# A state-space layer in an fp32 encoder kernel: an order written out by hand, splits and sums on VectorE, and rows by channel

## The chip, the cores and the metric

The kernel runs on one core of a Trainium2 chip. The metric is the device time of one execution in microseconds, as the median of several runs.

## What is computed

A trunk of two layers over a sequence of 512 positions with width 1024. Layer 0 mixes by dilated window attention, layer 1 by a bidirectional diagonal state-space layer (S5) with a gated output; after each mixer stands a SwiGLU feed-forward net, and a final RMS norm ends it. Only the second mixer is touched here:

```python
def s5_mixer(hn, w_in, a_re, a_im, log_dt, b_re, b_im, c_re, c_im, d_skip, w_glu):
    u = (hn @ w_in).reshape(b, s, SSM_GROUPS, SSM_GROUP_CH)      # 64 groups of 16 channels
    y = d_skip * u
    for direction in range(2):                                   # a scan each way, 64 complex states a group
        y = y + s5_direction(u, a_re[direction], ..., reverse=(direction == 1))
    ag = jax.nn.gelu(y.reshape(b, s, SSM_WIDTH)) @ w_glu
    return ag[..., :D_MODEL] * jax.nn.sigmoid(ag[..., D_MODEL:])
```

## The kernel before

**Matmuls.** Every fp32 weight is split into two fp32r numbers, hi and lo, and a product is made of three matmuls: hi by hi, lo by hi, hi by lo. Class `WStream` streams the weights in units of 128x1024: SP issues the load into `wraw`, three units ahead; ScalarE copies it to `whi` and `lo_engine` subtracts to get `wlo` (L108 to L117), two units ahead. `lo_engine` is VectorE, but in the state-space layer GpSimd. A unit is one DMA, except in the GLU: full units are made of four loads each (L93), half units, which hold both output parts for half of the input rows, of eight (L88).

**Tables.** The state-space layer works on chunks of eight positions, so that the recurrence over a chunk is a matmul with tables. These (`Ti` for the input, `Bt` for the output, `Mt` for what stays within a chunk, `ph` with cosine and sine of the phase) are built ahead, from about 615 to 963 us, as background pieces between the matmuls of layer 0's feed-forward net. `elem_in` (L432 to L442) makes a half tile of `Tn` in two pieces of three VectorE operations; TensorE transposes it and it goes to DRAM. The state-space layer loads the tables back, tile by tile, two buffers each.

**The state-space layer.** Eight tiles T of 128 channels (8 groups of 16). For each:

- `sps`: the projection, 24 matmuls; VectorE scales it to `u` (`s_u`, L1415); `s_move` (L1419) scatters `u` into `U` with eight 32-KB DMAs on SP, so that a group's chunk positions and channels are partitions.
- `V`: 64 small matmuls of U with `Ti` (L1308).
- `s_scan` (L1316 to L1341): four VectorE mults with `ph`, two GpSimd sums, two VectorE scans (the recurrence), four mults and two GpSimd sums, giving `xx`.
- `s_R` (L1350, L1352): four ScalarE copies of `xx` to `x`, shifted by a chunk, the second direction reversed.
- `s_O`: yps, matmuls of `Mt` with U and `Bt` with x (L1373, L1375); gelu on ScalarE (L1380).
- `s_tr`: per pair of tiles, eight transposes, then the split into `yh` and `yl`.

Then the GLU: eight output tiles of two parts. For the last four (`LATE`), `glu_part` makes the products with the first half of y while the last tiles are still in the scan, and a ScalarE copy (`gpart`, L1479) keeps them; at the end VectorE adds both halves (L1522). Gate, residual and square sums follow (L1529 to L1531, L1098 to L1101), and `msps` (L1106) begins the norm of the next feed-forward net.

The order of instructions is the order of the code on each engine; nothing is rescheduled. With V(T) the code puts the scan of T and the loads of `Ti` for T+2 on their queues; `ph`, then `Mt` and `Bt` for T+1 follow on SP behind Ti. The strides of `w_ssm_in` (channel within group outermost) are taken up when the weight is split (the `swap` units, L113 and L114).

Of the kernel before, what the change touches and what calls it, by code (L numbers as in the profile page):

```python
# [13 lines left out]
P = 128  # L14
S = 512
# [55 lines left out]
class WStream:  # L71


    def __init__(self, k, units, swap, pool, la, sa):
        self.k, self.units, self.swap, self.pool, self.la, self.sa = k, units, swap, pool, la, sa
        self.nl = self.ns = self.n = 0
        self.raw, self.hl = {}, {}
        self.lo_engine = k.nc.vector
# [21 lines left out]
    def split_to(self, n):  # L100
        nc = self.k.nc
        while self.ns <= min(n, len(self.units) - 1):
# [6 lines left out]
            if self.ns in self.swap:  # L109

                src = w.rearrange("p a (g c) -> p a c g", c=16)
                h4, l4 = (t.rearrange("p (a c g) -> p a c g", a=a, c=16) for t in (hv, lv))
                nc.scalar.activation(out=h4, in_=src, func=ACTF.Copy)  # L113
                self.lo_engine.tensor_tensor(out=l4, in0=src, in1=fv(h4), op=ALU.subtract)  # L114
            else:
                nc.scalar.activation(out=hv, in_=wv, func=ACTF.Copy)  # L116
                self.lo_engine.tensor_tensor(out=lv, in0=wv, in1=fv(hv), op=ALU.subtract)  # L117
# [63 lines left out]
class Tables:  # L181
# [5 lines left out]
    def __init__(self, k, a, cst, ident, pool, dram, rho):  # L187
# [8 lines left out]
        self.MD = [dram.tile([8, 16, 8, 128], F32, name=f"MD{t}") for t in range(KT)]  # L196
# [236 lines left out]
    def elem_in(self, T, s, i):  # L433
# [29 lines left out]
    def tr_in(self, T, s, q):  # L463
# [78 lines left out]
def build(tc, a, out):  # L542
# [45 lines left out]
    swap = range(len(units), len(units) + KT)  # L588
# [31 lines left out]
    with ExitStack() as ctx:  # L620
# [4 lines left out]
        ws = WStream(k, units, swap, wpool, 3, 2)  # L625
# [659 lines left out]
        pY = s0.enter_context(tc.tile_pool(name="psY", bufs=2, space=PSUM))  # L1285
# [30 lines left out]
        def s_scan(T):  # L1316
# [3 lines left out]
            V = vt.pop(T)  # L1320
            Vr, Vi = (V[:, i].rearrange("p g j -> p (g j)") for i in range(2))
            tl = lambda n, b=1: sp.tile([P, S], F32, tag=n, name=n, bufs=b)
            W = []
            for A_, B_, op in ((Vr, Vi, ALU.add), (Vi, Vr, ALU.subtract)):
                t1, t2 = tl("t1", 2), tl("t2", 2)
                nc.vector.tensor_tensor(out=t1, in0=A_, in1=C, op=ALU.mult)
                nc.vector.tensor_tensor(out=t2, in0=B_, in1=Sn, op=ALU.mult)
                nc.gpsimd.tensor_tensor(out=t1, in0=t1, in1=t2, op=op)
                W.append(t1)
            Q = []  # L1330
            for i in range(2):
                q = W[i]
                nc.vector.tensor_tensor_scan(out=q, data0=rho, data1=W[i], initial=0.0, op0=ALU.mult, op1=ALU.add)
                Q.append(q)
            xx[T] = []
            for i, (A_, B_, op) in enumerate(((Q[0], Q[1], ALU.subtract), (Q[1], Q[0], ALU.add))):
                x, t2 = Yp.tile([P, S], F32, tag=("sq", "acc")[i], name="xx", bufs=1), tl("t2", 2)
# [5 lines left out]
        xx = {}  # L1343

        def s_R(T):
# [9 lines left out]
            xs_[T] = R  # L1355

# [26 lines left out]
        def s_tr(t2):  # L1383
# [256 lines left out]
```

## Time and profile before

| what | value |
|---|---|
| runs | 1630.33, 1623.66, 1632.44 us; median 1630.33 |
| the profiled execution | 1624.28 us, span 1622.4 us |
| TensorE busy | 94% of the span, granted clock 0.979 on average |
| VectorE, ScalarE, GpSimd busy | 60%, 41%, 28% |
| HBM | 154 MB read, 27 MB written |

The busy shares are of the whole span; the change lies in the stretch from about 1040 to 1258 us, and in the background pieces from 615 to 963 us. The rows of those stretches follow below. A row of a wait gives who waited, on which line, for whom; a group row gives busy time, the mean of one instruction, and the idle time just before them.

### The profile page before, as it was taken

What the parts mean: (1) busy time and instruction counts of PE and PEld (TensorE: products, weight loads), DVE (VectorE), ACT (ScalarE), POOL (GpSimd) and SP (SyncE); (2) the same over time, 40 slices, a digit from 0 to 9 for tenths busy, and PEclk for the clock granted to TensorE, in tenths of its full rate; (3) what the DMA queues carried; (4) which work ended last, traced back from release to release, by engine and by line L of the source; (5) the groups of instructions that cost most, each with busy time, mean ns of one, the idle gap of its engine ahead of it and who ended that gap; (6) DMA issues with size and microseconds to landing.
All of it is one profiled execution on the core that took longest, in us unless ns stands there. A gap on an engine that the chain in (4) does not pass through costs nothing. (4 is left out here: it accounts for less than half of the span.)

```text
span 1622.4 us, 22425 instructions
## 1 busy us (share of the span) xinstructions
PE 1527.7 (94%) x8428; PEld 1261.1 (78%) x8428; DVE 976.6 (60%) x1721; ACT 660.6 (41%) x1172; POOL 452.5 (28%) x535
## 2 busy tenths in 40 slices
PE   8999999999998889799999999887799999999997
PEld 6887888898897668677777777776587888888886
DVE  6366665665666478888578875486547443344234
ACT  5265454454564323244344444442433333233122
POOL 1022001010110250387666754464413101101010
PEclk9999999999999899999999999998999999999999
DMA  6322232231222033355566547467623332333332
GB/s 185 91 78 58 62 92 64 78 87 58 90 68 66 29 86 91 84 143 146 166 194 175 163 145 253 146 223 218 210 70 88 104 103 80 104 98 98 105 102 65
DMA packets 279180, 185.16 MB, mean 114 GB/s; under 512 B 39936, under 2 KB 261280, under 8 KB 277024
## 3 DMA queue, kind: packets, MB, share of 16 engines
q1 hardware_dynamic: 278640, 183.13, 38.3%
q8 instruction: 66, 1.08, 0.3%
q10 hardware_dynamic: 432, 0.60, 0.1%
q14 instruction: 42, 0.34, 0.1%
HBM read 154.34 MB, written 27.26 MB: 112 GB/s over the span
## 5 line engine op out<-in xcount | busy, mean ns | idle before, releaser
L117 DVE TENSOR_TENSOR wlo<-wraw,whi 128x1024 fp32r<-128x1024 f32 (+1 forms) x232 | 312.1, 1349 | 192.7 <-ACT whi L116 191.0
L116 ACT ACTIVATE whi<-wraw 128x1024 fp32r<-128x1024 f32 x238 | 241.1, 1018 | 236.1 <-PE ops L1599 74.3
L789 PE MATMUL gps<-xhi,whi 128*128 128x512 f32 x792 | 320.2, 404 | 9.5 <-DVE hl L1206 6.5
L789 PE MATMUL gps<-xhi,wlo 128*128 128x512 f32 x792 | 311.9, 394 | 7.0 <-DVE wlo L117 7.0
L789 PE MATMUL gps<-xlo,whi 128*128 128x512 f32 x792 | 310.6, 392 | 0.5 <-DVE xlo L649 0.5
L983 POOL COPY st<-st 32x4 f32<-32x4 f32 x256 | 59.7, 233 | 453.9 <-ACT P L971 337.9
L789 PEld LDWEIGHTS gps<-xhi,wlo 128*128 128x128 f32 x792 | 149.3, 189 | 43.7 <-DVE wlo L117 11.2
L789 PEld LDWEIGHTS gps<-xhi,whi 128*128 128x128 f32 x792 | 149.6, 189 | 39.7 <-ACT whi L116 10.0
L789 PEld LDWEIGHTS gps<-xlo,whi 128*128 128x128 f32 x792 | 149.9, 189 | 26.0 <-DVE xlo L649 0.8
L789 PE MATMUL ups<-xhi,wlo 128*128 128x512 f32 x352 | 138.1, 392 | 2.0 <-DVE wlo L117 2.0
L789 PE MATMUL ups<-xhi,whi 128*128 128x512 f32 x352 | 139.6, 397 | 0.0
L789 PE MATMUL ups<-xlo,whi 128*128 128x512 f32 x352 | 137.7, 391 | 0.0
L971 ACT ACTIVATE P<-P,st 128x256 f32<-128x256 f32 x128 | 63.8, 499 | 68.7 <-DVE st L968 68.6
L1202 POOL TENSOR_TENSOR u<-u,g 128x512 f32<-128x512 f32 x22 | 28.4, 1291 | 209.7 <-DVE u L1200 202.2
L789 PEld LDWEIGHTS ups<-xhi,wlo 128*128 128x128 f32 x352 | 66.4, 189 | 17.0 <-DVE wlo L117 2.8
L452 POOL TENSOR_TENSOR B<-pout,C 128x512 f32<-128x512 f32 x32 | 45.3, 1415 | 122.4 <-DVE pout L178 64.3
L789 PEld LDWEIGHTS ups<-xhi,whi 128*128 128x128 f32 x352 | 66.5, 189 | 14.5 <-issue 1.2
L789 PEld LDWEIGHTS ups<-xlo,whi 128*128 128x128 f32 x352 | 66.6, 189 | 13.4
L1199 ACT ACTIVATE g<-g 128x512 f32<-128x512 f32 x44 | 27.7, 630 | 115.2 <-DVE g L1198 115.2
L789 PE MATMUL fps<-hh,whi 128*128 128x512 f32 x176 | 71.4, 406 | 3.4 <-ACT hh L1205 2.7
L891 PE MATMUL vps<-whi,xhi 128*128 128x256 f32 x256 | 73.3, 286 | 0.0
L1205 ACT ACTIVATE hh<-u 128x512 fp32r<-128x512 f32 x44 | 27.8, 633 | 109.9 <-POOL u L1202 87.7
(303 smaller groups left out, 3163.1 us busy)
## 6 DMA issues: line engine op xcount, KB each, us to landing
wraw<-in_w_ffn_in SPq DMA_DIRECT2D x88, 512.0 KB, 3.8
wraw<-in_w_qkv SPq DMA_DIRECT2D x72, 512.0 KB, 3.6
wraw<-in_w_ffn_out SPq DMA_DIRECT2D x38, 512.0 KB, 4.0
BD<-B SPq DMA_DIRECT2D x16, 512.0 KB, 5.3
TinD<-Tt SPq DMA_DIRECT2D x16, 512.0 KB, 3.5
Ti<-TinD SPq DMA_DIRECT2D x8, 1024.0 KB, 6.0
Bt<-BD SPq DMA_DIRECT2D x8, 1024.0 KB, 7.3
wraw<-in_w_attn_out SPq DMA_DIRECT2D x8, 512.0 KB, 3.8
```

The lines of the kernel that those rows point to most:

```text
L116: nc.scalar.activation(out=hv, in_=wv, func=ACTF.Copy)
L117: self.lo_engine.tensor_tensor(out=lv, in0=wv, in1=fv(hv), op=ALU.subtract)
L452: tt(out=B[:, i], in0=self.bc(self.pout, i, g0), in1=self.ch(C[:, 0]), op=ALU.mult)
L789: nc.tensor.matmul(dst, w[:, kt, :], x, start=(start and kt == ks[0] and j == 0), stop=(stop and kt == ks[-1] and j == 2))
L891: nc.tensor.matmul(ps[rp][:, r % 2, :], x, w[:, kk, :], start=(kt == 0 and j == 0 and r % 2 == 0), stop=(kt == 7 and j == 2 and r % 2 == 1))
L971: nc.scalar.activation(out=Pt[:, j, :], in_=Pt[:, j, :], func=ACTF.Exp, bias=st[:, 32 + off + j:33 + off + j], accum_out=st[:, 8 + off + j ...
L983: nc.gpsimd.tensor_copy(par[32 * z:32 * z + 32, y, :, :], own[32 * y:32 * y + 32, z, :, :])
L1199: nc.scalar.activation(out=g, in_=g, func=ACTF.Silu)
L1202: eng.tensor_tensor(out=u, in0=u, in1=g, op=ALU.mult)
L1205: nc.scalar.activation(out=hi, in_=u, func=ACTF.Copy)
```

## The change

- Weight splits stay on VectorE throughout; no `swap` units any more.
- u's rows in U run by channel, then by position in the chunk. `s_u` writes the eight positions in reverse, `s_move` has one DMA for each group (so V of a group needs one DMA only), and the tables are laid out to match: `elem_in` writes `Tn` with the position innermost and reads `pin` (a power of the state matrix, position outermost in memory) with a step of 512 bytes.
- `s_scan` is cut into `s_pre` and `s_post`; three of its four sums are on VectorE, some second operands lie in PSUM (`pU`), and only the second x sum is on GpSimd.
- `ph` of T+2 is loaded by ScalarE's DMA queue at the end of `s_R(T)`; Ti of T+2 is issued right after V(T); Mt and Bt of T+2 after the moves.
- The calls stand in one list. Transposes are made in two halves with one bank of PSUM and copied back in place. Six output tiles of the GLU instead of four are half done ahead, cut in parts between the other steps.

The core of the diff (the added scaling of `first`, the GLU banks and plain renamings are left out):

```diff
-            if self.ns in self.swap:
-                src = w.rearrange("p a (g c) -> p a c g", c=16)
...
+            nc.scalar.activation(out=hv, in_=wv, func=ACTF.Copy)
+            self.lo_engine.tensor_tensor(out=lv, in0=wv, in1=fv(hv), op=ALU.subtract)
...
-        tt(out=o, in0=self.bc(self.pin, 0, g0), in1=self.ch(bb[:, i]), op=ALU.mult)
-        tt(out=t, in0=self.bc(self.pin, 1, g0), in1=self.ch(bb[:, 1 - i]), op=ALU.mult)
+        pw = [self.pin[:, :, j, g0:g0 + 4].rearrange("p l (g o) -> p g o l", o=1).to_broadcast([P, 4, 16, 8]) for j in range(2)]
+        b = [bb[:, j].rearrange("p g (c o) -> p g c o", o=1).to_broadcast([P, 4, 16, 8]) for j in range(2)]
+        tt(out=o, in0=pw[0], in1=b[i], op=ALU.mult)
+        tt(out=t, in0=pw[1], in1=b[1 - i], op=ALU.mult)
...
-    LATE = range(4, KT)
+    LATE = range(2, KT)
...
-        def s_scan(T):
+        def s_pre(T):
...
             for A_, B_, op in ((Vr, Vi, ALU.add), (Vi, Vr, ALU.subtract)):
-                t1, t2 = tl("t1", 2), tl("t2", 2)
+                t1 = sp.tile([P, S], F32, tag="t1", name="t1", bufs=2)
+                t2 = pU.tile([P, S], F32, tag="t", name="t2p")
                 nc.vector.tensor_tensor(out=t1, in0=A_, in1=C, op=ALU.mult)
                 nc.vector.tensor_tensor(out=t2, in0=B_, in1=Sn, op=ALU.mult)
-                nc.gpsimd.tensor_tensor(out=t1, in0=t1, in1=t2, op=op)
...
+            for t1, t2, op in W:
+                nc.vector.tensor_tensor(out=t1, in0=t1, in1=t2, op=op)
+            for t1, _, _ in W:
+                nc.vector.tensor_tensor_scan(out=t1, data0=rho, data1=t1, initial=0.0, op0=ALU.mult, op1=ALU.add)
...
+        def s_post(T):
...
-                nc.gpsimd.tensor_tensor(out=x, in0=x, in1=t2, op=op)
+                (nc.vector, nc.gpsimd)[i].tensor_tensor(out=x, in0=x, in1=t2, op=op)
...
+            if T + 2 < KT:
+                load_tab(T + 2, "ph", eng=nc.scalar)
...
-            nc.vector.tensor_tensor(out=us[T], in0=ps, in1=rB, op=ALU.mult)
+            nc.vector.tensor_tensor(out=bass.AP(tensor=u.tensor, offset=u.offset + 448, ap=[list(u.ap[0]), [-64, 8], [1, 64]]),
+                                    in0=v(ps), in1=v(rB), op=ALU.mult)
...
-                nc.sync.dma_start(out=Us[T % 3][112 - 16 * l:128 - 16 * l, :, 1:65], in_=us[T][:, 64 * l:64 * l + 64])
+                nc.sync.dma_start(out=Us[T % 3][:, g, 1:65], in_=us[T][16 * g:16 * g + 16].rearrange("c (l j) -> c l j", l=8))
...
+        run((s_su, 2), (s_move, 2), (s_g, 3, 0), (s_V, 0), (s_pre, 0), (s_g, 3, 1), (s_su, 3), (s_post, 0), (s_V, 1), (s_pre, 1),
+            (s_g, 4), (s_su, 4), (s_g, 5), (s_R, 0), (s_O, 0), (s_post, 1), (s_V, 2), (s_pre, 2), (s_su, 5),
+            (s_g, 6), (s_R, 1), (s_O, 1), (s_post, 2), (s_V, 3), (s_pre, 3), (s_su, 6),
+            (s_tr, 0, 0), (s_g, 7, 0), (s_tr, 0, 1), (s_g, 7, 1), (s_R, 2), (s_O, 2), (s_post, 3),
+            (s_V, 4), (s_pre, 4), (s_su, 7), (s_R, 3), (s_O, 3), (s_V, 5), (s_tr, 1, 0), (s_tr, 1, 1),
+            (s_post, 4), (s_pre, 5), (next, fill[0]), (next, fill[0]), (next, fill[1]), (s_R, 4), (s_O, 4),
+            (s_V, 6), (s_post, 5), (s_pre, 6), (next, fill[1]), (next, fill[2]), (s_R, 5), (s_O, 5), (s_V, 7),
+            (s_tr, 2, 0), (next, fill[2]), (s_tr, 2, 1), (s_post, 6), (s_pre, 7), (next, fill[3]), (s_R, 6), (s_O, 6),
+            (s_post, 7), (next, fill[3]), (next, fill[4]), (next, fill[4]),
+            (s_R, 7), (s_O, 7), (next, fill[5]), (s_tr, 3, 0), (next, fill[5]), (s_tr, 3, 1))
```

Three places show how the instructions moved. **VectorE, the scan of tile 1**, before (`t` are the scan's operands, `xx` its result):

```order
L1415 TENSOR_TENSOR u<-sps_9704,rsB_9588 128x512
L1326 TENSOR_TENSOR t_9777<-V,ph 128x512
L1327 TENSOR_TENSOR t_9778<-V,ph 128x512
L1326 TENSOR_TENSOR t_9782<-V,ph 128x512
L1327 TENSOR_TENSOR t_9783<-V,ph 128x512
L1333 SCALAR_TENSOR_TENSOR t_9777<-rr_9494,t_9777 128x512
L1333 SCALAR_TENSOR_TENSOR t_9782<-rr_9494,t_9782 128x512
L1338 TENSOR_TENSOR xx<-t_9777,ph 128x512
L1339 TENSOR_TENSOR t_9790<-t_9782,ph 128x512
L1338 TENSOR_TENSOR xx<-t_9782,ph 128x512
L1339 TENSOR_TENSOR t_9795<-t_9777,ph 128x512
```

and now, where `t2p` is an operand in PSUM:

```order
L1322 TENSOR_TENSOR t_9776<-V,ph 128x512
L1323 TENSOR_TENSOR t2p<-V,ph 128x512
L1322 TENSOR_TENSOR t_9780<-V,ph 128x512
L1323 TENSOR_TENSOR t2p<-V,ph 128x512
L1327 TENSOR_TENSOR t_9776<-t_9776,t2p 128x512
L1327 TENSOR_TENSOR t_9780<-t_9780,t2p 128x512
L1329 SCALAR_TENSOR_TENSOR t_9776<-rr_9497,t_9776 128x512
L1329 SCALAR_TENSOR_TENSOR t_9780<-rr_9497,t_9780 128x512
L110 TENSOR_TENSOR wlo<-wraw,whi 128x1024
L1427 TENSOR_TENSOR u<-sps_9794,rsB_9591 128x8x64
L110 TENSOR_TENSOR wlo<-wraw,whi 128x1024
```

The two sums (L1327) are now between the mults and the scans, and two weight splits (`wlo`) and the scaling of a later tile stand between the scans and the mults behind them, which before came at once.

**SP, the queue around the loads for tile 5**, before (`wraw` are half units of the GLU, `U<-u` moves):

```order
L88 DMA wraw<-in_w_glu 64x2x128 x8
L1251 DMA Ti<-TinD_5462 128x2048
L1251 DMA ph<-PhD_5477 128x1024
L1419 DMA U_9486<-u 16x8x64 x8
L1251 DMA Mt<-MD_5485 128x1024
L1251 DMA Bt<-BD_5469 128x2048
```

and now, at the same number of moves:

```order
L88 DMA wraw<-in_w_glu 64x2x128 x8
L1433 DMA U_9488<-u 128x1x64 x8
L1246 DMA Mt<-MD_5484 128x1024
L1246 DMA Bt<-BD_5468 128x2048
L1246 DMA Ti<-TinD_5462 128x2048
L88 DMA wraw<-in_w_glu 64x2x128 x8
```

`ph` has left the queue, and `Ti` of tile 5 (TinD_5462) now comes behind the moves of tile 4 and the tables Mt and Bt of tile 3 instead of ahead of moves and tables.

**ScalarE around the copies of tile 4**, before (`x<-xx` are the copies, `rr` an operand of the scan of a later tile):

```order
L116 ACTIVATE whi<-wraw 128x1024
L1391 ACTIVATE yh_10332<-yt 128x512
L1391 ACTIVATE yh_10336<-yt 128x512
L1350 ACTIVATE x_10340<-xx 64x512
L1352 ACTIVATE x_10340<-xx 64x512
L1350 ACTIVATE x_10343<-xx 64x512
L1352 ACTIVATE x_10343<-xx 64x512
L1314 ACTIVATE rr_9494<-rho 128x8x63
```

and now:

```order
L1394 ACTIVATE ys<-yt 128x512 x2
L1400 ACTIVATE yh_10369<-ys 128x512
L1400 ACTIVATE yh_10373<-ys 128x512
L109 ACTIVATE whi<-wraw 128x1024
L1457 ACTIVATE gpart<-pe 128x512 x2
L109 ACTIVATE whi<-wraw 128x1024
L1457 ACTIVATE gpart<-pe 128x512
L1352 ACTIVATE x_10470<-xx 64x512
L1354 ACTIVATE x_10470<-xx 64x512
L1352 ACTIVATE x_10473<-xx 64x512
L1354 ACTIVATE x_10473<-xx 64x512
L1246 DMA ph<-PhD_5479 128x1024
```

Now two weight copies and three copies of half tiles stand ahead of the x copies, and the load of ph behind them.

## Rows read from the trace of the kernel before

**Rows 1.** busy time by stretch, 1040 to 1240; stretch, its length, busy us (x instructions) by engine, PEclk, DMA share, GB/s

```profile
1140.00:1160.00 20.00, 12.42 (x101) 10.07 (x102) 12.98 (x15) 5.62 (x10) 12.50 (x8) 0.83 0.78 248
...
sum 200.00, PE 170.56 PEld 142.56 DVE 118.44 ACT 71.53 POOL 77.59; mean PE 17.06 PEld 14.26 DVE 11.84 ACT 7.15 POOL 7.76
```

**Rows 2.** waits of TensorE, 1020 to 1265: total us, times, longest us

```profile
PE yps L1375 <- ACT x L1352: 17.8, 12, 5.3
PE pe L789 <- ACT gpart L1479: 7.6, 1, 7.6
PE V L1308 <- DMA U<-u: 3.5, 1, 3.5
```

**Rows 3.** VectorE's groups, 1040 to 1180: busy us, mean ns, idle before and releasers

```profile
L1333 DVE TENSOR_TENSOR_SCAN t<-rr,t 128x512 f32<-128x512 f32 x16 | 26.8, 1713 | 9.9 <-ACT rr L1314 5.1 <-POOL t L1328 4.7
L1339 DVE TENSOR_TENSOR t<-t,ph 128x512 f32<-128x512 f32 x16 | 19.5, 1220 | 0.0
L1326 DVE TENSOR_TENSOR t<-V,ph 128x512 f32<-128x512 f32 x16 | 10.9, 683 | 20.6 <-DMA ph<-PhD 16.6 <-PE V L1308 4.0
...
L1338 DVE TENSOR_TENSOR xx<-t,ph 128x512 f32<-128x512 f32 x16 | 10.7, 669 | 0.0
```

**Rows 4.** waits of ScalarE, 1040 to 1180

```profile
ACT whi L116 <- DMA wraw<-in_w_glu: 31.1, 4, 13.1
```

**Rows 5.** SP's DMA issues in order of time: start, us, engine, line

```profile
1090.64 8.85 SPq L88 DMA_DIRECT2D wraw<-in_w_glu  x8
1099.59 0.54 SPq L1251 DMA_DIRECT2D Ti<-TinD  x1
1100.22 0.38 SPq L1251 DMA_DIRECT2D ph<-PhD  x1
```

**Rows 6.** the page's costliest groups: VectorE's weight splits

```profile
L117 DVE TENSOR_TENSOR wlo<-wraw,whi 128x1024 fp32r<-128x1024 f32 (+1 forms) x232 | 312.1, 1349 | 192.7 <-ACT whi L116 191.0
```

**Rows 7.** groups of GpSimd and ScalarE, 1040 to 1180

```profile
L1340 POOL TENSOR_TENSOR xx<-xx,t 128x512 f32<-128x512 f32 x16 | 22.8, 1423 | 34.1 <-DVE t L1339 33.3 <-PE sps L789 0.7
...
L1352 ACT ACTIVATE x<-xx 64x512 f32<-64x512 f32 x16 | 10.0, 627 | 0.2
```

**Rows 8.** TensorE in order of time: start, us

```profile
1177.75 1.07 PE L1375 MATMUL yps<-Bt,x 128*64 128x128 f32 x8
...
1179.66 0.39 PE L789 MATMUL pe<-yh,wlo 128*128 128x512 f32 x1
1179.89 0.40 PE L789 MATMUL pe<-yh,whi 128*128 128x512 f32 x1
...
1183.30 1.03 PE L1386 MATMUL yt<-cst,ys 128*128 128x128 f32 x8
...
1223.63 0.39 PE L789 MATMUL pg<-yh,whi 128*128 128x512 f32 x1
...
1257.89 1.05 PE L1106 MATMUL msps<-ones,acc 128*128 128x1 f32 x8 [1.56 <-POOL acc L1101]
```

**Rows 9.** VectorE in order of time, the GLU's half tiles

```profile
1229.76 1.27 DVE L1522 TENSOR_TENSOR gpart<-pg,gpart 128x512 f32<-128x512 f32 x2
...
1237.04 1.27 DVE L1522 TENSOR_TENSOR gpart<-pg,gpart 128x512 f32<-128x512 f32 x2
...
1251.59 1.27 DVE L1522 TENSOR_TENSOR gpart<-pg,gpart 128x512 f32<-128x512 f32 x2
```

**Rows 10.** VectorE's groups, 640 to 1000: a table mult

```profile
L440 DVE TENSOR_TENSOR Tn<-pin,bbP 128x512 f32<-128x512 f32 x32 | 21.7, 678 | 0.4 <-ACT bb L431 0.4
```

**Rows 11.** VectorE in order of time: a plain and a strided weight split

```profile
1000.42 1.22 DVE L117 TENSOR_TENSOR wlo<-wraw,whi 128x1024 fp32r<-128x1024 f32 x1 [1.36 <-ACT whi L116]
...
1023.95 1.98 DVE L114 TENSOR_TENSOR wlo<-wraw,whi 128x1024 fp32r<-128x1024 f32 x1 [0.96 <-ACT whi L113]
```

**Rows 12.** busy time by stretch, 615 to 800 and 800 to 963, summed

```profile
sum 348.00, PE 331.62 PEld 259.75 DVE 281.47 ACT 136.73 POOL 206.06; mean PE 165.81 PEld 129.87 DVE 140.74 ACT 68.37 POOL 103.03
```

**Rows 13.** waits of TensorE, 640 to 1000

```profile
PE gps L789 <- DVE wlo L117: 5.5, 7, 1.7
```

More of the change, by code (lines that the diff above doesn't have):

```diff
@@ L195, in __init__ @@
         self.PhD = [dram.tile([P, 2, S], F32, name=f"PhD{t}") for t in range(KT)]
-        self.MD = [dram.tile([8, 16, 8, 128], F32, name=f"MD{t}") for t in range(KT)]
+        self.MD = [dram.tile([16, 8, 8, 128], F32, name=f"MD{t}") for t in range(KT)]
         self.z, self.C = {}, {}
@@ L606, in glu_half @@
                       for u in range(2) for g in range(2) for part in range(2)])
-    LATE = range(4, KT)
+    LATE = range(2, KT)
     for m in LATE:
         glu_half(m, 0)
-    for m in range(4):
+    for m in range(LATE[0]):
         glu_full(m)
@@ L1326, in s_scan @@
                 nc.vector.tensor_tensor(out=t1, in0=A_, in1=C, op=ALU.mult)
                 nc.vector.tensor_tensor(out=t2, in0=B_, in1=Sn, op=ALU.mult)
-                nc.gpsimd.tensor_tensor(out=t1, in0=t1, in1=t2, op=op)
[L1329 to L1334, printed above, removed]
+                W.append((t1, t2, op))
@@ L1335, in s_scan @@
+            vt.pop(T)
+            for t1, t2, op in W:
+                nc.vector.tensor_tensor(out=t1, in0=t1, in1=t2, op=op)
+            for t1, _, _ in W:
+                nc.vector.tensor_tensor_scan(out=t1, data0=rho, data1=t1, initial=0.0, op0=ALU.mult, op1=ALU.add)
+            Qs[T] = [w[0] for w in W]
+        def s_post(T):
+            ph = ld[T]["ph"]
+            C, Sn = ph[:, 0, :], ph[:, 1, :]
+            Q = Qs.pop(T)
             xx[T] = []
             for i, (A_, B_, op) in enumerate(((Q[0], Q[1], ALU.subtract), (Q[1], Q[0], ALU.add))):
[L1337 removed]
+                x = Yp.tile([P, S], F32, tag=("sq", "acc")[i], name="xx", bufs=1)
+                t2 = sp.tile([P, S], F32, tag="t2", name="t2", bufs=2) if i else pU.tile([P, S], F32, tag="t", name="t2p")
@@ L1411, in build, with s_V, s_O @@
+        def s_V(T):
+            s_rho(T)
+            for g in range(8):
+                s_v(T, g)
+            if T + 2 < KT:
+                load_tab(T + 2, "Ti")
+        def s_O(T):
+            for q in range(4):
+                s_out(T, q)
+            s_gelu(T)
+            if T + 3 < KT:
+                s_move(T + 3)
+            if T + 2 < KT:
+                load_tab(T + 2, "Mt", "Bt")
         us = {}
@@ new lines, in s_move, with s_g @@
+        def s_move(T):
+            for g in range(8):
+                nc.sync.dma_start(out=Us[T % 3][:, g, 1:65], in_=us[T][16 * g:16 * g + 16].rearrange("c (l j) -> c l j", l=8))
+        gps, rB = {}, []
+        def s_g(T, part=None, hook=None):
+            if part != 1:
+                gps[T] = (ws.get(), (pT if T == 2 else p1).tile([P, S], F32, tag="yt" if T == 2 else "f", name="sps2"))
+            wl, ps = gps[T]
+            ks = {None: range(KT), 0: range(KT // 2), 1: range(KT // 2, KT)}[part]
+            gemm_a(Z, ps, wl=wl, ks=ks, start=part != 1, stop=part != 0, hook=hook)
```

191 lines of the change are left out of this document (58 added, 133 removed).

## The prediction

> **What bounds it now.** I read the page's first table (TensorE busy 94% of the span), then busy time by stretch. Outside the state-space stage TensorE hardly pauses. Inside it, from 1040 to 1180, its busy time falls to 12.42 of 20 us and its granted clock to 0.83 [rows 1]: the lower of its two levels, 1.2 GHz, for part of the stretch, right after it had stood idle. The sum over 1040 to 1240 is 170.56 us busy in 200, so 29.4 us of TensorE stand still.
>
> The waits of TensorE say for what: 17.8 us for the state copies x that ScalarE makes, in 12 pieces (5.3 us the longest), 7.6 us once for a half-tile copy, 3.5 us once for moved u [rows 2]. The copies are only the last link. One step back, on VectorE, the first mult of a tile's scan waited 16.6 us for `ph`, in four pieces, 5.1 us for `rr` from ScalarE and 4.7 us for a sum from GpSimd [rows 3]. On ScalarE a weight copy waited 31.1 us for its load, with rr and x queued behind it [rows 4]. Both start at SP: at 1090.64 eight GLU loads take 8.85 us to issue, then come Ti and, only at 1100.22, ph [rows 5]. So the stage is bound by a chain SP, VectorE, GpSimd, ScalarE, TensorE, once per tile.
>
> **The change, term by term.** Let X be the end of the last tile's yps: before, 1177.75 + 1.07 = 1178.8 [rows 8].
>
> 1. *ph from ScalarE's queue.* It is issued behind the x copies of two tiles earlier, so a tile ahead of its use. The 16.6 us should go. ScalarE pays six issues; none of its issues is in the trace, so each costs between 0 and SP's 0.38 [rows 5], at most 2.3 us. They stand ahead of the gelu, which waits for yps anyway, so I cost them at nothing; without that cover it is the 2.3 us.
>
> 2. *Splits and sums on VectorE.* What the chain then costs is VectorE's own time per tile. From rows 3: before the split point four mults with V (0.68 each, starts 0.60 apart in a row), two sums taken as such an op, two scans of 1.71: 6 x 0.61 + 3.43 = 7.1 us. After it four mults and one sum at 0.61 to 0.67, about 3.2 us. L1339 means 1.22 beside L1338's 0.67: the second of each tile shares its time with a GpSimd sum, and with three of four sums gone from GpSimd I count it at 0.67 for most. Per tile that is 10.3 us, for eight 82 us. To this come eight weight splits between the scans of tile 0 and the last x (the order on VectorE, above, shows two of them), at 1.35 [rows 6], 10.8 us; five u at 0.68, 3.4 us; six yl, also 0.68, 4.1 us. Together 100 us. V(0)'s 3.5 us wait [rows 2] should go, since each group's V waits for its own move only and half a projection stands ahead of it; so VectorE can begin near 1052. 1052 + 100 = 1152; one GpSimd sum of 1.4, two x copies of 0.63 [rows 7] and the outputs (four blocks like the last of rows 8, some 2.5) give **X = 1158** if VectorE never waits. That is the lower end.
>
> 3. *The new waits.* The upper end is X = 1178, where it stands. ScalarE's 31.1 us of waiting for GLU loads [rows 4] is not removed: the half units come through SP as eight loads each, six of them before X instead of four, at 8.85/8 = 1.1 us per load where the lanes are full [rows 5]. In the new order the copies of such units stand on ScalarE ahead of the x copies of tiles 4 and 6, and half-tile copies ahead of those of tiles 4 to 7. SP's own list loses six ph issues (2.3 us) and gains 16 loads before X. So one or two of these late weights will still push a tile. Nothing in the trace says by how much; I take the middle, **X = 1168**, a gain of 10.8 us. What else is moved past SP (moves by channel, eight of 32 KB as before; Ti now ahead of the moves) I cost at nothing: its cover is the two-tile lead, and if that is gone a move is a V wait like the 3.5 us above.
>
> 4. *Six half tiles.* After X TensorE has the sixth half tile, the last transposes and the GLU: four full tiles and four halves before, two full and six halves now. A half tile is 24 matmuls of 0.227 (the starts of two neighbours in rows 8), 5.45 us, a full one 10.9. But half tiles leave VectorE and ScalarE only every 1237.04 - 1229.76 = 7.28 us [rows 9], so from the second on this sets the pace. From X: 5.45 + 1.0 (transposes, rows 8) + 21.8 for the full ones; 6.2 to the first half tile's sum (its first matmul began at 1223.63 [rows 8], the sum at 1229.76); 5 x 7.28 to the sixth's; and 1257.89 - 1251.59 = 6.3 [rows 8, 9] to the square sum `msps`. Together 77.2 us; before it was 1257.89 - 1178.8 = 79.1. Gain **1.9 us**: two half tiles are off TensorE there, 10.9 us, and the chain eats most. The copies that the transposes gain (0.6 us each, like the x copies) lie on this path for the last pair alone, under the sixth half tile; without that cover they are 1.2 us more.
>
> 5. *Rows by channel.* The eight strided weight splits become plain ones; they gave TensorE no wait. The table-building pieces pay instead: 64 VectorE mults, now 0.68 [rows 10], read `pin` with a 512-byte step in the innermost axis. The nearest row is VectorE's strided split of weights, 1.98 us beside 1.22 for the plain one [rows 11]: 0.76 more for 1024 elements, 0.38 for 512. 64 x 0.38 = 24 us more VectorE work, in a stretch where it is busy 281 of 348 us [rows 12]. Lower bound 0 (the other operand is a broadcast, which may leave room), upper bound 24, all of it exposed. Most is hidden, since TensorE's weights are split two units ahead; what isn't hidden is what delays a split that is late already: TensorE waited 5.5 us for them in seven pieces [rows 13]. Two pieces of table, four strided mults, stand ahead of a split at most, 1.5 us. I take **3 us**, two such waits lengthened.
>
> Sum: -10.8 - 1.9 + 3 = -9.7 on the profiled 1624.28 gives 1614.6. That execution lies near the lowest of the runs shown; with them (1623.66, 1630.33, 1632.44) the mean of four is 1627.7, 3.4 above it. So I forecast **1618 us**. The median of 1630.33 less 0.5% (8.2 us, about what a measurement can tell from no change) is 1622.2.
>
> **The rivals.**
>
> A. *VectorE is the only bound.* X = 1158 and no table cost: -20.8 - 1.9 = -22.7, with 3.4 again 1605. For it: the ph wait is the largest single one and plainly goes. Against: 31.1 us of late weights.
>
> B. *The late weight takes ph's place.* SP is issuing back to back, so the x copies of tiles 4 to 6 stand behind GLU loads as scan mults waited for ph. X = 1177, and the table costs its 3 us: -1.8 - 1.9 + 3 = -0.7: 1627. For it: one cause, SP, stood behind both waits. Against: ph no longer stands in that queue, and the order puts plain work ahead.
>
> C. *The strided table reads come out.* Each strided mult is 0.38 longer, so each block of two pieces (there are 16) delays the split behind it by 1.5 us, and TensorE waits as much more wherever the split had no slack. It decides from 0.75 us a block: 16 x 0.75 = 12 us is the 3.7 us of gain with X near 1177, and 8.2 over. At 1.0 us a block it is 1627.7 - 3.7 + 16 = 1640; with X = 1168 it is 1631. For it: VectorE is busy 81% of that stretch, and splits are late seven times already. Against: these waits sum to 5.5 us today, and splits are made two units ahead.
> The Trainium skill ("Advanced Engine Details and Errata", section Memory Cachelines) says that SBUF reads which hit a different 16-byte line at each access pay a penalty; that speaks against this change. The trace agrees in kind: 1.98 against 1.22 us [rows 11]. The page gives no size, so the sum goes by the row.
>
> D. *The change does not shorten the chain*: TensorE's written-out order itself waits, for instance a half tile for its one psum copy as in the 7.6 us [rows 2]. It gives B's time, and I count it there.
>
> **Chances.** Forecast (X between 1163 and 1173): 0.38. A: 0.19. B with D: 0.26. C: 0.17. Faster by over 0.5%: all of A and three quarters of the forecast, 0.47. Within 0.5%: the rest of the forecast and B, 0.35. Slower: C's, with the end of B, 0.18. The range goes from a little under A, for the spread of the runs, 1602, to between C's two times, 1636. The likeliest case alone spans 1613 to 1623.
>
> **What would show it.** Right: no wait of VectorE's scan mult for ph; GpSimd's share down by the splits and three sums; last yps near 1168; half tiles every 7.3 us to the end; table mults near 1.06 us. Wrong: yps still waiting some 15 us for x with whi behind in_w_glu (B); TensorE waits for wlo between 640 and 1000 above 15 us (C); TensorE never below 18 of 20 us in the stage (A).

## The result, and the profile after

The changed kernel takes 1678.52 us (median of four runs, 1670.69 to 1678.94) beside 1629.88 for the kernel before (now four runs): a ratio of 1.0301, with a 95% interval of 1.0275 to 1.0326. It is 49 us slower; the forecast was 1618, with a range from 1602 to 1636. The profiled execution took 1678.76 us, its span is 1677.0.

To see where the time went I cut both traces at four instructions: the first hh copy of layer 0's feed-forward net (hh is the hi part of its hidden values), the first V, the end of the last yps, and msps after the GLU. What comes before the first differs by at most 5.3 us between all these executions, what comes behind the last by 1.7. The later runs stand in the same table (their edits are told below); the ratio is to runs of the kernel before on the same chip.

| kernel | hh to first V: tables, projections | V to last yps: scan stage | to msps: tail | ratio (95%) |
|---|---|---|---|---|
| before | 433.4 | 128.7 | 79.1 | 1 |
| after | 456.7 | 147.5 | 89.4 | 1.0301 (1.0275 to 1.0326) |
| e1 pin plain | 438.6 | 145.5 | 89.3 | 1.0193 (1.0166 to 1.0220) |
| e2 before, strided | 455.1 | 123.9 | 79.2 | 1.0126 (1.0101 to 1.0151) |
| e3 adds behind | 451.6 | 142.9 | 77.2 | 1.0225 (1.0192 to 1.0258) |
| e4 half tiles' splits late | 456.4 | 139.7 | 90.1 | 1.0275 (1.0249 to 1.0302) |
| e5 splits on GpSimd | 453.1 | 149.7 | 90.2 | 1.0315 (1.0291 to 1.0340) |
| e6 ph on SP | 450.3 | 150.0 | 90.1 | 1.0311 (1.0284 to 1.0339) |
| e7 post first | 453.0 | 146.0 | 90.9 | 1.0288 (1.0254 to 1.0323) |
| e8 all splits late | 458.6 | 145.6 | 89.5 | 1.0296 (1.0262 to 1.0329) |
| e9 Ti behind | 451.5 | 145.8 | 89.4 | 1.0296 (1.0266 to 1.0327) |
| c1 five edits | 436.1 | 133.8 | 77.0 | 1.0044 (1.0027 to 1.0061) |
| c2 and post of tile 4 first | 436.5 | 133.1 | 77.0 | 1.0041 (1.0026 to 1.0057) |
| c3 c1 with four halves | 438.8 | 127.4 | 80.4 | 1.0039 (1.0025 to 1.0052) |
| e10 MD on GpSimd | 460.1 | 142.7 | 90.2 | 1.0319 (1.0294 to 1.0343) |
| c4 c1, MD on GpSimd | 445.2 | 133.4 | 77.3 | 1.0068 (1.0045 to 1.0092) |
| c5 before, MD on GpSimd | 444.6 | 128.9 | 78.8 | 1.0068 (1.0044 to 1.0092) |
| e11 MD stores later | 449.4 | 145.1 | 89.4 | 1.0275 (1.0243 to 1.0306) |
| c6 c1, MD stores later | 431.5 | 133.8 | 77.5 | 1.0000 (0.9986 to 1.0015) |
| c7 before, MD stores later | 427.8 | 125.3 | 78.8 | 0.9954 (0.9937 to 0.9970) |

A column is one execution. Stretches of the same code differ between executions: the first one takes 450 to 459 us where nothing in it was edited (after, e3, e4, e6 to e9), the second 143 to 148 (after, e1, e3, e10, e11). So a column shows what a stage lost only to within 5 to 8 us, and a verdict on less is the ratio's. One execution of e9 took 3054.72 us at full clock, for no reason that the record shows; its ratio rests on the other three.

All three stretches are longer: +23.3, +18.8 and +10.3. Of the first, 2.7 us are work that was moved in, the half projection that now stands ahead of V(0) (12 matmuls of 0.227). In that stretch the table mults answer to [rows 10]; the groups of VectorE, 640 to 1040, of the changed kernel:

```profile
L436 DVE TENSOR_TENSOR Tn<-pin,bbP 128x512 f32<-128x512 f32 x32 | 34.6, 1081 | 0.5 <-ACT bb L424 0.5
L437 DVE TENSOR_TENSOR tm<-pin,bbP 128x512 f32<-128x512 f32 x32 | 34.3, 1073 | 0.0
```

1.08 us against 0.68, 32 of each. TensorE's waits between 690 and 1040, after the change (total us, times, longest; gps and fps are the feed-forward net's gate and output matmuls, tps and eps those of the tables):

```profile
PE gps L784 <- DVE wlo L110: 7.2, 6, 1.9
PE gps L784 <- ACT whi L109: 5.2, 3, 3.4
PE fps L784 <- DVE wlo L110: 4.0, 5, 1.3
PE fps L784 <- ACT whi L109: 3.6, 4, 1.5
PE fps L784 <- ACT hh L1200: 3.2, 1, 3.2
PE tps L466 <- DVE Tn L438: 2.4, 2, 2.2
PE eps L475 <- ACT Tt L467: 1.9, 2, 1.0
```

and in the same part of the program (690 to 1025) of the kernel before, those for split weights:

```profile
PE gps L789 <- DVE wlo L117: 3.7, 4, 1.7
PE fps L789 <- DVE wlo L117: 2.9, 3, 1.1
...
PE gps L789 <- ACT whi L116: 1.2, 1, 1.2
PE fps L789 <- ACT whi L116: 0.6, 1, 0.6
```

In all the kernel before waits 11.3 us there, 6.6 of them for wlo and 1.8 for whi, the copy on ScalarE; here it is 27.5, with 11.2 for wlo and 8.8 for whi.

In the scan stage no wait for ph is left: the first mults of the scans wait for V alone ([rows 3] have 16.6 us for ph):

```profile
L1322 DVE TENSOR_TENSOR t<-V,ph 128x512 f32<-128x512 f32 x16 | 10.9, 683 | 7.7 <-PE V L1304 7.7
```

The waits of TensorE from 1060 to 1330 ([rows 2]):

```profile
PE yps L1380 <- ACT x L1354: 34.0, 14, 10.5
PE pg L784 <- DVE gpart L1501: 14.1, 2, 8.4
```

The waits for x have doubled, from 17.8 to 34.0. The two longest are one place each. ScalarE in order of time (the idle time before an instruction, and what ended it, stands in brackets):

```profile
1099.36 1.06 ACT L109 ACTIVATE whi<-wraw 128x1024 fp32r<-128x1024 f32 x1 [7.13 <-DMA wraw<-in_w_ssm_in]
...
1100.32 0.61 ACT L1352 ACTIVATE x<-xx 64x512 f32<-64x512 f32 x1
...
1168.09 1.06 ACT L109 ACTIVATE whi<-wraw 128x1024 fp32r<-128x1024 f32 x1 [10.23 <-DMA wraw<-in_w_glu]
...
1169.53 0.62 ACT L1352 ACTIVATE x<-xx 64x512 f32<-64x512 f32 x1
```

and SP's issues ahead of the first of them:

```profile
1087.73 1.00 SPq L1246 DMA_DIRECT2D Ti<-TinD  x2
1088.85 0.38 SPq L96 DMA_DIRECT2D wraw<-in_w_ssm_in  x1
```

The last projection's weight is issued at 1088.85, behind two Ti of 1 MB; it lands 10.4 us later, the copy whi runs at 1099.36, and only then x of tile 0: TensorE stood still for 7.0 us. At 1168.09 it is a GLU half unit in front of tile 4's x, and TensorE stood still for 10.5 us.

Busy time by stretch (length, busy us of TensorE, its weight loads, VectorE, ScalarE and GpSimd, granted clock, DMA share, GB/s), from the first V to the last yps and from there to msps, of the changed kernel:

```profile
1076.00:1224.00 148.00, 111.08 (x1151) 93.17 (x1152) 90.98 (x126) 50.94 (x78) 10.23 (x8) 0.86 0.57 184
1224.00:1313.00 89.00, 74.91 (x316) 60.99 (x314) 48.79 (x50) 27.18 (x36) 19.60 (x15) 0.90 0.23 66
```

and of the kernel before:

```profile
1050.00:1179.00 129.00, 103.60 (x1137) 87.22 (x1138) 84.20 (x93) 47.16 (x70) 63.01 (x40) 0.90 0.67 206
1179.00:1258.00 79.00, 76.51 (x339) 62.78 (x340) 46.60 (x47) 26.56 (x33) 19.61 (x15) 1.00 0.28 81
```

TensorE is idle for 36.9 us of the stage (148 - 111.08), 25.4 before: 11.5 of the 18.8 us. 2.7 are work that was moved in, a fifth half tile (5.45) less the half projection that now stands ahead of V(0) (2.7). The rest, 4.6 us, I put down to the clock: a mean granted clock of 0.86 beside 0.90 means some 41 us at the lower level, 1.2 GHz (2 x 0.14 x 148), beside 26, in a stage with more stops. VectorE is busy 61% of it; e5, below, takes the splits off it and wins nothing.

The tail has 5.45 us of work less (the sixth half tile ahead is in it) and is 10.3 longer: TensorE is idle for 14.1 us of it beside 2.5, and the clock is 0.90 beside 1.00. Its half tiles ([rows 9]), VectorE:

```profile
1257.73 1.27 DVE L1501 TENSOR_TENSOR gpart<-pg,gpart 128x512 f32<-128x512 f32 x2
...
1264.97 0.68 DVE L1501 TENSOR_TENSOR gpart<-pg,gpart 128x512 f32<-128x512 f32 x1
1270.83 0.69 DVE L1501 TENSOR_TENSOR gpart<-pg,gpart 128x512 f32<-128x512 f32 x1 [5.18 <-PE pg L784]
...
1277.53 1.27 DVE L1501 TENSOR_TENSOR gpart<-pg,gpart 128x512 f32<-128x512 f32 x2
```

and TensorE there:

```profile
1265.71 0.79 PE L784 MATMUL pg<-yh,whi 128*128 128x512 f32 x1 [5.72 <-DVE gpart L1501]
...
1292.78 0.80 PE L784 MATMUL pg<-yh,whi 128*128 128x512 f32 x1 [8.37 <-DVE gpart L1501]
```

At 1264.97 one add stands alone, the second follows at 1270.83: from 1264.97 to the next tile's adds at 1277.53 it is 12.6 us instead of 7.28, and once more, with the wait at 1292.78, 12.7.

### The profile page after: what moved, and what is told of

Read it like the earlier page. It is cut to its first block, busy times and chain, and to the rows that moved or that the text cites. A ratio compares the mean times of both kernels' runs of the same rounds, so it can differ in the third digit from the quotient of the medians.

```text
span 1677.0 us, 22457 instructions
## 1 busy us (share of the span) xinstructions
PE 1546.1 (92%) x8428; PEld 1272.8 (76%) x8428; DVE 1009.7 (60%) x1760; ACT 660.6 (39%) x1184; POOL 388.5 (23%) x500
## 3 DMA queue, kind: packets, MB, share of 16 engines
q8 instruction: 66, 1.08, 0.3%
## 5 line engine op out<-in xcount | busy, mean ns | idle before, releaser
L110 DVE TENSOR_TENSOR wlo<-wraw,whi 128x1024 fp32r<-128x1024 f32 (+1 forms) x245 | 327.8, 1342 | 224.2 <-ACT whi L109 222.6
L109 ACT ACTIVATE whi<-wraw 128x1024 fp32r<-128x1024 f32 x246 | 249.5, 1019 | 256.9 <-PE ops L1578 74.3
L1194 ACT ACTIVATE g<-g 128x512 f32<-128x512 f32 x44 | 27.7, 630 | 128.9 <-DVE g L1193 128.9
L784 PE MATMUL fps<-hh,wlo 128*128 128x512 f32 x176 | 70.2, 399 | 5.5 <-DVE wlo L110 5.5
L1201 DVE TENSOR_TENSOR hl<-u,hh 128x512 fp32r<-128x512 f32 x44 | 35.8, 813 | 63.4 <-ACT hh L1200 63.4
```

The costliest lines, as they stand in the source:

```text
L784: nc.tensor.matmul(dst, w[:, kt, :], x, start=(start and kt == ks[0] and j == 0), stop=(stop and kt == ks[-1] and j == 2))
L1194: nc.scalar.activation(out=g, in_=g, func=ACTF.Silu)
L1201: nc.vector.tensor_tensor(out=lo, in0=u, in1=fv(hi), op=ALU.subtract)
```

## The experiments

**Theory 1: the strided reads.** e1 stores pin with the position innermost, by the same instructions:

```diff
-        self.pin, self.pout = self.t("pin", [8, 2, 64]), self.t("pout", [8, 2, 64])
+        self.pin, self.pout = self.t("pin", [2, 64, 8]), self.t("pout", [8, 2, 64])
...
-            V.tensor_copy(self.pin[0:64, 1:8, i, :], pw[i][0:64, 0:7])
+            V.tensor_copy(self.pin[0:64, i, :, 1:8].rearrange("p g l -> p l g"), pw[i][0:64, 0:7])
...
-        pw = [self.pin[:, :, j, g0:g0 + 4].rearrange("p l (g o) -> p g o l", o=1).to_broadcast([P, 4, 16, 8]) for j in range(2)]
+        pw = [self.pin[:, j, g0:g0 + 4, :].rearrange("p g (o l) -> p g o l", o=1).to_broadcast([P, 4, 16, 8]) for j in range(2)]
```

> The changed kernel with pin stored position innermost, so that the 64 table mults read it with a step of one element; everything else as changed. Theory 1 (the strided reads cost what was lost before 1040 us: 64 mults at 1.08 instead of 0.68 us, nothing of it hidden): mults back at 0.68 us and about 25 us less, near 1654. Rival 1 (the reads were hidden, and what was lost there comes from something else in rows by channel, the transposes or the table DMAs): mults at 0.68 us, time within 5 us of 1678.

Measured: the mults take 0.68 us again:

```profile
L436 DVE TENSOR_TENSOR Tn<-pin,bbP 128x512 f32<-128x512 f32 x32 | 21.7, 678 | 0.5 <-ACT bb L424 0.5
```

The time is 1658.83 us; the ratio falls by 0.0108, 17.6 us. e2 puts the strided operands (the added lines of elem_in in the change, written into the old tile) into the kernel before:

> The kernel before with only the operands of the 64 table mults changed to the strided ones; the order of the table's elements is then another one than the rest of the kernel takes, so the layer's values differ, not its work. Theory 1: mults at 1.08 us and 20 to 25 us more than before, near 1652. Rival 1: within 5 us of 1630.

Measured: 1645.62 us, 1.26% or 20.5 us more than before, all in the first stretch (+21.7). Its two groups of mults:

```profile
L443 DVE TENSOR_TENSOR Tn<-pin,bbP 128x512 f32<-128x512 f32 x32 | 34.5, 1079 | 0.5 <-ACT bb L431 0.5
L444 DVE TENSOR_TENSOR tm<-pin,bbP 128x512 f32<-128x512 f32 x32 | 34.4, 1075 | 0.0
```

So one and the same part is worth 18 us taken away and 20 added. 25.2 us of work were added on VectorE (68.9 for the two groups less 43.7 with plain reads), and 70 to 80% of it is paid. Theory 1 stands, rival 1 is out; the size was 7 us under what e1 expected and at the lower end for e2.

**Theory 2: the adds.** For output tiles 3 and 6 both parts lie in one PSUM tile (pV), and the code wrote the add of part 0 ahead of the matmuls of part 1. e3:

```diff
                 for part in range(2):
                     gemm_a(Yl[4:], pp[part], wl=tuple(w[:, :, part * 128:part * 128 + 128] for w in wl), ks=range(4))
+                for part in range(2):
                     t = parts.pop((m, part))
                     nc.vector.tensor_tensor(out=t, in0=pp[part], in1=t, op=ALU.add)
```

> The changed kernel with both matmul groups of a half tile written ahead of its two adds. Theory 2 (for output tiles 3 and 6, whose two parts lie in one PSUM tile, the second group waits for the first add: TensorE's waits of 5.7 and 8.4 us for gpart): half tiles every 7.3 us throughout, about 10.5 us less, near 1668. Rival 2 (VectorE's and ScalarE's chain of 7.3 us sets the end anyway, and the waits lie beside it): under 3 us less.

Measured: 1663.54 us, 0.0076 or 12 us less (10.5 expected); the tail is 77.2 us. VectorE's adds:

```profile
1248.38 1.27 DVE L1502 TENSOR_TENSOR gpart<-pg,gpart 128x512 f32<-128x512 f32 x2
...
1255.65 1.27 DVE L1502 TENSOR_TENSOR gpart<-pg,gpart 128x512 f32<-128x512 f32 x2
...
1262.93 1.27 DVE L1502 TENSOR_TENSOR gpart<-pg,gpart 128x512 f32<-128x512 f32 x2
```

Every step is 7.28 us now, and both waits for gpart are gone. Nothing but the place of the adds was changed, so what the matmuls of part 1 waited for was the add that reads part 0 of the same tile, though the two parts share no word.

**Theory 3: late weights in ScalarE's queue.** e4 splits the half tiles' weights one unit ahead instead of two:

```diff
-            hi, lo = ws.get()
+            hi, lo = ws.get(ahead=1)
```

> The changed kernel with the weights of the half tiles done ahead split one unit ahead instead of two, so that a late GLU load no longer stands on ScalarE in front of the x copies of tile 4. Theory 3 (late weights in the in-order queues are what the scan stage lost: TensorE's longest wait for x, 10.5 us at 1170, goes): 8 to 12 us less, near 1668. Rival 3 (the tile is late for another reason, Ti or the moves, and the wait only changes its name): within 3 us of 1678. Slower is possible too if TensorE then waits for splits: up to 5 us more.

Measured: the wait of 10.5 us at tile 4 is gone, the stage 7.8 us shorter in its profile; 1672.23 us, a ratio 0.0026 lower, 4 us with intervals that overlap. That the late unit caused this wait is shown; that it cost the 8 to 12 us expected is not. e8 does the same with the last three projections (`ws.get(ahead=1 if T > 4 else None)`):

> The run with the half tiles' weights split one unit ahead, and the last three projections' weights too, so that no late weight copy stands on ScalarE in front of the x copies of tile 0. Theory 3: TensorE's first long wait for x (7 us) goes as the second did, and the stage from the first V to the last yps is near the 129 us of before: 15 to 18 us less than the change, near 1661. Rival 6 (tile 0's x are late by the scan, not by the weight): the wait stays, near 1672.

Measured: both long waits are gone, TensorE's sum for x falls to 16.7 us, and the time stays (1.0296), where 15 to 18 us less were expected. In their place stand 5.3 us for a wlo that is now split too late and 6.2 for U: TensorE's waits in the stage fall only from 37.0 to 32.0 us in all. e9 takes the other end, the order on SP:

```diff
+            if 1 < T and T + 2 < KT:
                 load_tab(T + 2, "Ti")
...
-            (s_g, 4), (s_su, 4), ...
+            (s_g, 4), (load_tab, 2, "Ti"), (load_tab, 3, "Ti"), (s_su, 4), ...
```

> The changed kernel with the loads of Ti for tiles 2 and 3 (1 MB each) behind the load of the last projection's weight instead of ahead of it on SP; nothing else. Theory 3: that weight landed 10.4 us after its issue because of them, and its copy stands on ScalarE in front of tile 0's x; TensorE's wait there falls from 7.0 to 1 or 2 us, 4 to 6 us less in the stage. Rival 7: the weight is as late with the loads in the other order, or V(2) now waits for Ti: within 3 us of 1678.

Measured: tile 0's wait goes, and one of 6.8 us appears two tiles later, behind the copy of the next late GLU unit; 1.0296. A late transfer that is mended shows the next: the order holds several in a row, and no one of these three runs gives time clear of its interval.

**Rival 4 (VectorE's splits hold up the scan), and the other parts.** e5 sets `ws.lo_engine = nc.gpsimd` again for the stage:

> The changed kernel with the weight splits of the state-space stage (from projection 0 to the last half tile ahead) on GpSimd again. Theory 3 (late weight copies on ScalarE stand in front of x; the split behind them on VectorE is only in their wake): the waits of 7.0 and 10.5 us for x stay, 1678 within 4 us. Rival 4 (the split on VectorE, which waits for its weight copy, holds up the scan queued behind it): TensorE's waits for x shrink by 8 us or more in all and the time with them.

Measured: 1.0315, waits for x 31.4 us with 9.7 the longest. Having the splits on VectorE neither helped nor hurt here. e6 leaves out `eng=nc.scalar`:

> The changed kernel with ph loaded on SP's queue again, at the same place of the code. If loading by ScalarE is what took VectorE's waits for ph away, they come back in part, a few us to 10 us more. Rival: the place in the code (two tiles ahead) did it, not the queue: no wait for ph, within 3 us of 1678; and if the load on ScalarE's queue itself delayed the gelu, up to 4 us less.

Measured: VectorE waits for ph again, and the time is the same (1.0311 beside 1.0301):

```profile
DVE t L1322 <- DMA ph<-PhD: 12.7, 3, 5.8
```

In the changed kernel, which waits elsewhere, the wait for ph is covered. Whether it was covered in the kernel before too no run shows: none loads ph by ScalarE's queue there, or by SP's in c1. e7 moves `(s_post, 6), (s_pre, 7)` ahead of `(s_tr, 2, 0)`:

> The changed kernel with s_post and s_pre of tiles 6 and 7 ahead of the transposes of pair 2, so that yl on VectorE stands behind them and not in front; TensorE's own order is the same. Theory 5 (VectorE waited 11.1 us in front of yl at 1196 with the ready x of tile 6 behind it): x of tile 6 earlier by 8 to 10 us, and TensorE's waits at 1200 to 1203 (5.0 us) go: 3 to 6 us less. Rival: TensorE reaches tile 6's outputs no earlier, since half tiles fill its queue: within 2 us of 1678.

Measured: the waits of 2.8 and 2.2 us at tile 6 become 1.5 and 0.9, but the time is within its interval (1.0288): not settled.

**Together.** c1 has the edits of e1, e3, e4, e7 and e9.

> The changed kernel with all five edits: pin position innermost, both matmul groups of a half tile ahead of its adds, half tiles' weights split one unit ahead, post of tile 6 ahead of pair 2's transposes, Ti of tiles 2 and 3 behind the last projection's weight. If the three losses (table reads, late weights, adds) are separate, they add: 18 to 23 + 12 + 8 to 15 us less than 1678, so 1628 to 1640. If they hide one another, it stays above 1645.

Measured: 1632.88 us, 1.0044 (1.0027 to 1.0061): 42 of the 49 us are back, within what was expected if the three losses add. Stage and tail are 133.8 and 77.0. e1 and e3 alone gave 17.6 and 12.4 us, so by subtraction the three edits of the order gave some 12 together, an estimate that the intervals leave open by 9 either way. The busy time of c1's stage, and TensorE's waits for x:

```profile
1053.00:1187.00 134.00, 109.30 (x1150) 91.80 (x1148) 89.83 (x125) 49.79 (x77) 10.23 (x8) 0.90 0.64 199
```

```profile
PE yps L1380 <- ACT x L1354: 21.4, 14, 6.3
```

TensorE is idle for 24.7 us of it, beside 25.4 before, and waits 21.4 us for x, beside 17.8: even mended, the new order has none of the gain for which it was written. The longest wait, 6.3 us, is the late GLU unit that e9 brought up at tile 2. c2 also moves `(s_post, 4)` ahead of `(s_tr, 1, 0)`:

> The run with all five edits, and post of tile 4 ahead of pair 1's transposes, so that yl of pair 1 no longer stands before it on VectorE. If what is left of tile 4's wait comes from VectorE's order, 2 to 4 us less than with the five edits; if from SP's queue, no difference.

No difference. c3 has `LATE = range(4, KT)` and the calls of two fills left out:

> The run with all five edits, and four half tiles done ahead instead of six. Theory: two half tiles more are 10.9 us of TensorE moved from the tail, where the 7.3-us chain of VectorE and ScalarE takes most of it back, into the stage, where part of it falls into waits: with four, the tail is 5 to 8 us longer and the stage about as much shorter: within 4 us of the five edits. Rival: six halves fill waits that stay empty with four: 5 us or more slower with four.

Measured: 6.5 us less in the stage, 3.4 more in the tail (5 to 8 were expected), 1.0039: within the interval of c1. No gain of six halves over four is seen.

**By which route the tables' delay reaches TensorE (theory 8: through SP's queue).** SP waits 124.8 us in front of the MD stores between 690 and 1040 (102.6 before), for VectorE, and weight loads queue behind. e10, c4 and c5 issue those 64 stores from GpSimd's queue (`self.nc.gpsimd.dma_start`) in the changed, the mended and the kernel before:

> The changed kernel with the 64 stores of the within-chunk table (MD) issued from GpSimd's queue instead of SP's. Theory 8 (the late VectorE reaches TensorE by way of SP: the store waits for E on VectorE, the weight load queued behind it is late, and so is ScalarE's copy): TensorE's waits for whi and wlo between 690 and 1050 fall by 8 us or more, 8 to 15 us less than the change. Rival 8 (the split itself stands behind the mults on VectorE): waits for wlo stay, under 4 us less.

> The run with all five edits, and the 64 stores of MD on GpSimd's queue. If the same route costs something with plain table reads too, 3 to 8 us less than with the five edits, so at or below the kernel before; if VectorE in time leaves SP nothing to wait for, no difference.

> The kernel before with nothing but the 64 stores of MD on GpSimd's queue. Theory 8: its 7 us of waits for split weights between 690 and 1025 shrink, 2 to 6 us less than before. Rival 8: no difference; GpSimd's own issue of them could cost 1 or 2 us.

What theory 8 forecast came in none of the three: they take 1.0319, 1.0068 and 1.0068, that is 3, 4 and 11 us more than without the edit (the first two within their intervals). In e10 TensorE's waits for whi and wlo between 690 and 1040 did fall, from 20.0 to 7.7 us, but 11.7 us for the copy of a transposed table (Tt) and 5.4 for hl, the lo part of the hidden values, came up. GpSimd itself now waits in the stores for VectorE (86.2 us in e10), and SP waits for GpSimd's ph (72.9 us, 5.7 before the edit). The wait only changed its queue. e11, c6 and c7 leave the queue and move the stores behind weight loads:

```diff
-                u += behind[3:]
+                u += behind[3:4]
...
+                u += behind[4:]
                 u.append((400, lambda T=T, s=s: self.store_out(T, s)))
```

> The changed kernel with the MD stores four pieces later in the background list, still on SP, so that one or two weight loads a half block stand ahead of them and no longer behind; engines, their orders and the work are otherwise the same. Theory 8 (SP waits in the store for VectorE and holds up the weight load behind it): SP's waits in front of MD fall below half of 125 us, TensorE's waits for whi and wlo between 690 and 1050 shrink by 8 us or more, 8 to 15 us less than the change. Rival 8 (the split itself stands behind the longer mults on VectorE): SP's waits fall, TensorE's don't, within 4 us of the change.

> The run with all five edits, and the MD stores later. Theory 8: 3 to 8 us less than with the five edits, near or below the kernel before (ratio 0.998 to 1.002). Rival 8: no difference (1.004).

> The kernel before with nothing but the MD stores later. Theory 8: its waits for split weights between 690 and 1025 shrink, 3 to 6 us less than before (ratio 0.996 to 0.998). Rival 8: no difference.

Measured: e11 takes 0.0026 less than the change, 4 us with intervals that overlap. SP's waits in front of the MD stores fall from 124.8 to 76.2 us, not below half. Its waits of TensorE from 690 to 1040 are

```profile
PE eps L475 <- ACT Tt L467: 9.4, 5, 2.9
PE fps L785 <- DVE wlo L110: 3.1, 4, 1.5
PE fps L785 <- ACT hh L1201: 3.0, 1, 3.0
PE tps L466 <- DVE Tn L438: 2.6, 2, 2.4
PE gps L785 <- DVE wlo L110: 2.3, 3, 1.0
PE fps L785 <- ACT whi L109: 1.7, 2, 1.1
```

where waits for whi and wlo have fallen from 20.0 to 7.1 us, as theory 8 said, and 9.4 us for Tt have come up instead. c6 is 0.0044 under c1 and level with the kernel before (1.0000); c7 is 0.9954 (0.9937 to 0.9970): 1618.75 us, 7 us faster than before and the best here. So with plain reads the route by SP is shown to cost 7 us, in c6 and in c7. How much of the 18 to 20 us of the strided reads takes this route is not shown: the 4 us of e11 lie within its noise, and the other ways were not parted.

## Why the prediction was wrong

1. *ph from ScalarE's queue*: right, the wait went. But the step took the 16.6 us for a price, and in the changed kernel e6 brings 12.7 of them back for nothing. ScalarE's six issues take 0.33 us each, 2.0 in all, inside the bound of 2.3; the trace of before does hold issues of ScalarE, unlike what the step says (one, at 0.73 us of the span, takes 0.38).
2. *Splits and sums on VectorE*: a scan took 1.21 us where I took 1.71, the mean of two kinds (below), so 8 us of the 100 were not there. As the lower end, 108 us from the first V to X, the step was not tested: the shortest such stage of a changed kernel is 127.4 us (c3). VectorE was not what the others waited for: with the splits on GpSimd the time is the same (e5).
3. *The new waits* is one step that failed. It named the mechanism and one of the places (a late weight copy ahead of tile 4's x), and then took the middle between "VectorE never waits" and "where it stands", as if the new order could not be worse than the old. The upper end left out tile 0, where the last projection's weight lands behind two Ti, and that each late unit holds up on ScalarE the x copies behind it, so that one order can lose several times. Forecast was X 10.8 us earlier; counted from the first V it came 18.8 later, 11.5 of it idle time and 2.7 moved work. In the profiles e4 gives back 8 us of the stage, and the three edits of the order together (c1) 14. The sign that I had set for rival B came, x waiting behind a whi for in_w_glu, and with 34.0 us twice as long as the 15 I named. The gain itself came in no run: mended (c1), the stage stands idle as long as before, and what bounds it there stays open.
4. *Six half tiles*: the sum was right to 0.1 us (77.2, e3 77.2), and the step still failed: 89.4. I counted what VectorE and ScalarE do but not that the two parts of tiles 3 and 6 are one tile, so that a matmul waits for the add before it. The gain of 1.9 us was in fact a loss of 10.3. And after the mend, six halves gave no gain over four that c3 could show.
5. *Rows by channel* is a term that was mis-sized: 3 us, measured 18 (e1) and 20 (e2). The mult's price was right (0.38 forecast, 0.40). Wrong was "Most is hidden, since TensorE's weights are split two units ahead". The lead is in units, and VectorE, SP and ScalarE work in order: the store waits for E behind both table pieces, the load behind the store, the copy behind the load. That this path costs time is shown for 7 us with plain reads (c6, c7); how the 18 to 20 divide between it and late splits on VectorE stays open. With VectorE at 81% of the stretch (now 82% of a longer one: 307.4 of 375 us) an added microsecond found little slack. The step also read too little in [rows 13], which are the gate's matmuls alone: with those of the output, and with whi, TensorE waited 9.9 us for split weights there, not 5.5. Rival C had it, "decides from 0.75 us a block"; it was 1.3 a block (20.5 / 16), above its higher price of 1.0. Its sign was set wrong all the same: between 640 and 1000 TensorE waited 12.1 us for wlo, under the 15 that I had named, and 15.0 for whi. The rule of the Trainium skill on reads that hit a new line at each access ("Advanced Engine Details and Errata", Memory Cachelines) held: 1.08 against 0.68 us, and 0.68 again with plain reads in e1.

The range ended at 1636: C was given 0.17, and its price stood alone there, not with the stage and the tail; no rival had two of the three losses at once.

## What to carry to other kernels

Here VectorE was busy four fifths of a stretch, and 70 to 80% of the work added to it there came out as time. Price an addition to such an engine near its whole length until a wait with slack is named instruction by instruction, through every in-order queue (store, load behind it, copy behind that). Before a tile of PSUM is split in two, see that no reader of one half stands in the program ahead of a writer of the other. And the longest wait in a profile need not be time: mending one late transfer moved the stall two tiles on (e9), mending two left the time as it was (e8), and of the 42 us that five edits gave back some 30 came from two edits that touched no transfer (e1, e3).

## What the runs showed of the hardware

In the kernel before, the first scan of a tile ran beside a GpSimd sum and took 2.28 to 2.30 us (1.85 for the last tile, where less of it ran beside one); the second, with none beside it, took 1.19. The mean of 1.71 in [rows 3] is of the two. After the change no scan has a GpSimd instruction beside it, and all sixteen take 1.19 to 1.22. The two scans of a tile, before and after:

```profile
1143.33 3.41 DVE L1333 TENSOR_TENSOR_SCAN t<-rr,t 128x512 f32<-128x512 f32 x2 [0.21 <-POOL t L1328]
```

```profile
1138.56 2.33 DVE L1329 TENSOR_TENSOR_SCAN t<-rr,t 128x512 f32<-128x512 f32 x2
```

I had not expected the scan to be longer beside GpSimd: it makes 8 us less of VectorE's time in the stage (16 x 0.5). The weight split in the stage takes 1.21 us instead of 1.35 over the kernel before [rows 6]. The groups of VectorE and of GpSimd from 1070 on, after the change:

```profile
L1329 DVE TENSOR_TENSOR_SCAN t<-rr,t 128x512 f32<-128x512 f32 x16 | 18.7, 1206 | 0.0
L110 DVE TENSOR_TENSOR wlo<-wraw,whi 128x1024 fp32r<-128x1024 f32 x11 | 13.3, 1213 | 25.3 <-ACT whi L109 25.3
```

```profile
L1342 POOL TENSOR_TENSOR xx<-xx,t 128x512 f32<-128x512 f32 x8 | 10.2, 1279 | 142.2 <-DVE t L1341 103.2 <-ACT x L1354 39.0
```

What stays open: with plain reads the first stretch is still 3 to 5 us longer than before (e1, c1 to c3). The half projection that was moved into it is 2.7 of them; the wait of 3.5 us for U in front of V(0) [rows 2] left the same stretch, so a few us remain unexplained, about what executions differ by.
